# Block two's operand from rows short of the norms' rstd, the overflow loop moved ahead, and two sets of fillers

## The chip, the cores and the metric

One core of a Trainium2 chip runs the kernel. It has TensorE (PE: matmuls and transposes), VectorE (DVE), ScalarE (ACT), GpSimd (POOL) and SyncE (SP, which issues the DMAs here). The metric is the device time of one execution in microseconds (us), lower is better.

## The reference, cut to what matters

Two blocks on 512 tokens of width 1024, all float32. Block one is a token mixer (short convolution and forgetting attention with 16 heads, both gated) and a two-level mixture of 32 experts; its last step is an RMS norm. Block two is an mLSTM and pooling layer, which begins with an RMS norm of its own, and then a latent attention layer with 8 heads.

```python
x = x + token_mixer(rmsnorm(x, norm_mix_g), ...)
x = x + hier_moe(rmsnorm(x, norm_ffn_g), ...)
return rmsnorm(x, norm_final_g)                  # end of block one
...
u = rms_norm(x, a_norm_g) @ a_w_in               # start of block two
xm, om, gates, zm, xp, zp = jnp.split(u, ...)
...
p = softmax(where(mask, q @ k.T * scale, -inf))  # latent attention, per head
o = (p @ v) * silu(z)
```

Two RMS norms follow each other at the seam: block two's operand is x times a factor per row (both norms' rstd) times a gain per column (norm_final_g times a_norm_g).

## The kernel before, in words

Each float32 operand of a dense product is split into a high part rounded to float32r (on ACT) and a low part (the difference, on DVE or POOL); `hilo` and `wsplit` do this, and `pair3` makes three matmuls of it. `dense_T` makes one 128 x 512 output tile from 24 such matmuls (8 blocks of k, three each) into a PSUM bank of the group `mm`. Weights come by DMA into tiles `raw`, and their two parts into two buffers `w`.

The instructions of an engine run in a fixed order that a planner wrote down ahead, with the program order as its first rule of choice and its own costs and waits. `pin` and `in_order` keep matmuls in program order; `no_sync_barrier` keeps all that stands behind it behind all that stands ahead; `issue_after` holds work back until a given instruction. `banks` says which PSUM banks a group (mm, tr, s, o, c) rotates over.

Attention of block one (`attention`) runs 8 pairs of heads, with scores in bank group s, `softmax_T` and value products (L452). Behind it `gate_att` makes 8 gate tiles with `dense_T` and a tanh on ACT (L477) into one tile `sg` whose pool is opened after attention's pool is closed. PE uses these gate products to fill its waits as far as banks allow.

Experts are run in 16 pairs (`experts`). The last steps there: the down products of pair 15 in two halves (`down_half`, L848), `combine` (L923, added to the rows X by DVE, L924) in two halves, and between them `overflow`, a loop with a count read from memory, which runs no iteration with these inputs (L1027, L1028). All five engines meet at it. Then `final_half` takes the statistics per tile and half: X times norm_final_g on POOL into `hs` (L947), the squares on ACT (L948, L951) or DVE (L953). `final_rows` makes both norms' rstd from them (L958 on), scales the rows (L967, L969), `front` transposes the scaled rows (L252) and splits them into the operand `hT` of block two, and POOL makes the new X from hs (L1173).

Block two's first part is `gates_m` (24 matmuls with 36 columns), `pool_branch` (8 pairs of dense tiles xp and zp) and `mlstm` (4 heads, each with two dense blocks om, two tiles xm, two tiles zm). An output of xp or xm is copied by ACT (L1248, L1291), one of zp or zm goes to `silu2` (tanh on ACT, product on DVE, L1180 and L1181). From xm the convolution on DVE (L1297) leads to xc, the operand of the q and k products.

In the latent attention `scores` makes 32 units (head, tile): a maximum on DVE (L1628), its product with the query's scale on DVE (mx, L1629), the exponential on ACT (L1632), the reciprocal on DVE (L1634) and the scaling of the row on DVE for even and on POOL for odd tiles (L1635); `values` transposes the result (L1649) and multiplies it with V (L1656). The weights uq and uk of the next heads are split in one piece each (L234, L235).

Of the kernel before, what the change touches and what calls it, by code (L numbers as in the profile page):

```python
# [19 lines left out]
P = 128  # L20
# [16 lines left out]
GATES_FIRST = 4  # L37
ROUTER_AT = (1, 2, 3, 4, 5, 6)
GAIN_ON_ACT = (0, 1)
# [6 lines left out]
class Program:  # L46
# [427 lines left out]
    def gate_att(self):  # L474
        for f in range(KB):
            pg = self.dense_T(self.hT)
            self.nc.scalar.activation(self.sg[:, f, :], pg, AF.Tanh, scale=0.5)  # L477

    def mix_out(self, pool):
        nc = self.nc  # L480
        sg = self.sg
        for f in range(KB):
            py = self.dense_T(self.by_k(self.B))
            m = pool.tile([P, T], F32, name="m2", bufs=2)
            nc.vector.scalar_tensor_tensor(m, sg[:, f, :], 1.0, py, op0=OP.add, op1=OP.mult)
# [308 lines left out]
    def experts(self):  # L794
# [133 lines left out]
    def begin_final(self, n):  # L928

        nc = self.nc  # L930
        s = [self.moe_slots[(n + i) % MOE_SLOTS]() for i in range(7)]
        two = lambda u: [u[:, 0:D], u[:, D:2 * D]]
        self.hs = two(s[0]) + two(s[1])
        self.rows = two(s[2]) + two(s[5])
        self.gfin, self.gfin2 = two(s[3])
        self.sq = [s[4][:, i * 512:(i + 1) * 512] for i in range(NT)]
        self.y_over = [x.bitcast(F32R) for x in two(s[6])]
        nc.sync.dma_start(self.gfin, self.a["norm_final_g"].to_broadcast([P, D]))
        nc.gpsimd.tensor_tensor(self.gfin2, self.gfin, self.gfin, op=OP.mult)
        self.ss = self.small.tile([P, 2, NT, 2], F32, name="s12", bufs=1)  # L940

    def final_half(self, t, half):

        nc = self.nc
        c = slice(half * 512, half * 512 + 512)
        x, q = self.X[:, t, c], self.sq[t]
        nc.gpsimd.tensor_tensor(self.hs[t][:, c], x, self.gfin[:, c], op=OP.mult)  # L947
        self.squared = nc.scalar.activation(q, x, AF.Square, accum_out=self.ss[:, half, t, 0:1])  # L948
        gain = self.ss[:, half, t, 1:2]
        if half == 0 and t in GAIN_ON_ACT:  # L950
            nc.scalar.activation(q, self.hs[t][:, c], AF.Square, accum_out=gain)  # L951
        else:
            nc.vector.scalar_tensor_tensor(q, q, 1.0, self.gfin2[:, c], op0=OP.mult, op1=OP.mult, accum_out=gain)  # L953

    def final_rows(self):

        nc = self.nc
        nc.vector.tensor_tensor(self.ss[:, 0], self.ss[:, 0], self.ss[:, 1], op=OP.add)  # L958
        v, w = (self.small.tile([P, NT, 2], F32, name="v12", bufs=1), self.small.tile([P, NT], F32, name="v2", bufs=1))
        nc.vector.tensor_scalar(v[:, :, 0], self.ss[:, 0, :, 0], 1.0 / D, EPS, op0=OP.mult, op1=OP.add)  # L960
        nc.vector.tensor_scalar(w, v[:, :, 0], EPS, None, op0=OP.mult)
        nc.vector.scalar_tensor_tensor(v[:, :, 1], self.ss[:, 0, :, 1], 1.0 / D, w, op0=OP.mult, op1=OP.add)
        r = self.rsqrt(v.rearrange("p t n -> p (t n)"), 8)
        for t in range(NT):
            g = r[:, 2 * t + 1:2 * t + 2]
            if t == 3:
                nc.scalar.activation(self.rows[t], self.hs[t], AF.Copy, scale=g)  # L967
            else:
                nc.vector.tensor_scalar(self.rows[t], self.hs[t], g, None, op0=OP.mult)  # L969
        self.rfin = r  # L970
# [123 lines left out]
    def block_one(self):  # L1094
# [6 lines left out]
        with ExitStack() as s1:  # L1101
# [20 lines left out]
            self.sg = sgp.tile([P, KB, T], F32, name="sg")  # L1122
            self.gate_att()
# [41 lines left out]
            self.expert_banks()  # L1165
            for _ in steps:
                pass
            self.final_rows()
            self.usual_banks()
            self.hT = self.by_k(self.B)  # L1170
            self.front(self.rows, self.hT, "a_norm_g")
            for t in range(NT):
                nc.gpsimd.tensor_scalar(self.X[:, t, :], self.hs[t], self.rfin[:, 2 * t:2 * t + 1], None, op0=OP.mult)  # L1173
# [3 lines left out]
    def silu2(self, pool, src, out):  # L1177

        nc = self.nc
        nc.scalar.activation(out, src, AF.Tanh, scale=0.5)  # L1180
        nc.vector.scalar_tensor_tensor(out, out, 1.0, src, op0=OP.add, op1=OP.mult)  # L1181

    def gates_m(self, pool, keep):
# [7 lines left out]
        for k in range(KB):  # L1191
            self.pair3(b[:36, :], (wgh[:, k, :], wgl[:, k, :]), self.hT[k],
                       k == 0, k == KB - 1)
        it, ft, e, cf, ones = (pool.tile([4, T], F32, name="gm_" + n) for n in ("i", "f", "e", "cf", "one"))
# [31 lines left out]
    def pool_branch(self, pool, first):  # L1226
# [11 lines left out]
        for g in range(4):  # L1238
# [4 lines left out]
            for j in range(2):  # L1243
# [4 lines left out]
                nc.scalar.copy(x[:, 16:], px)  # L1248
# [11 lines left out]
                self.silu2(pool, pz, sz[:, j, :])  # L1260
# [11 lines left out]
    def mlstm(self, pool):  # L1272
# [7 lines left out]
        for h in range(4):  # L1280
            th = pool.tile([P, NT, 256], F32, name="th_om", bufs=1)
            for u, b in self.two_blocks():
                nc.scalar.activation(th[:, 2 * u:2 * u + 2, :], b, AF.Tanh, scale=0.5)
# [21 lines left out]
            for j in range(2):  # L1305
                self.silu2(pool, self.dense_T(self.hT), sz[:, j, :])
# [108 lines left out]
    def block_two_a(self):  # L1415
        nc, tc = self.nc, self.tc
        with ExitStack() as s1:
# [105 lines left out]
    def mla_heads(self, p, keep, x3):  # L1523
# [4 lines left out]
        def q_tile(hp, t):  # L1528
            d = pairs[hp]
            if t == 0:  # L1530
# [4 lines left out]
                self.hilo(*d["uq"], w[:, :1152], lo_engine=nc.gpsimd if hp else None)  # L1535
# [11 lines left out]
        def kv_tile(hp, t):  # L1547
            d = pairs[hp]
            if t == 0:
# [4 lines left out]
                self.hilo(*d["uk"], w[:, :1024], lo_engine=nc.gpsimd if hp else None)  # L1554
# [63 lines left out]
        def scores(h, t):  # L1618
# [10 lines left out]
            nc.vector.tensor_tensor(mx, mx, qs, op=OP.mult)  # L1629
# [5 lines left out]
            (nc.gpsimd if t % 2 else nc.vector).tensor_scalar(pr[:, :nk], pr[:, :nk], rp, None, op0=OP.mult)  # L1635
# [113 lines left out]
VEC_NAMES = [("norm_mix_g", 8), ("norm_ffn_g", 8), ("conv_w0", 8), ("conv_w1", 8), ("conv_w2", 8), ("conv_b", 8), ("b_forget", 1),  # L1749
# [32 lines left out]
def layout(i):  # L1782
# [35 lines left out]
    vecs[:16, VEC_AT["b_forget"]] = i["b_forget"]  # L1818
    o["norm_final_g"] = i["norm_final_g"].reshape(1, D)
# [51 lines left out]
```

## Time and profile before

| what | value |
|---|---|
| median of 3 runs | 1791.58 us (1791.04 to 1791.61) |
| the profiled execution's own time | 1791.53 us |
| its span, first to last instruction | 1789.8 us |
| mean granted TensorE clock | 0.988 |
| busy: PE, DVE, ACT, POOL | 1718.7, 908.2, 616.0, 314.2 us |
| DMA moved | 321.35 MB |

Times in the profile count from the first instruction of the span. An engine's busy time leaves out its waits; where an engine sat idle, a timeline row gives in brackets how long, and which engine's instruction ended it. The granted clock is a share of TensorE's full speed: 1.00 is 2.4 GHz, 0.50 is 1.2 GHz.

### The profile page before, as it was taken

The page shows a single profiled execution, that of the slowest core. Times are in us where ns is not written, and L with a number is a line of the kernel's source. Part 1 is how long each engine was busy: PE and PEld are TensorE (multiplying, and loading weights), DVE is VectorE, ACT ScalarE, POOL GpSimd, SP SyncE. Part 2 cuts the span into 40 slices and gives each one's busy share as a digit, 9 for nine tenths or more (in the row PEclk, how much of TensorE's full clock was granted, in tenths as well). Part 3 has the DMA queues.
Part 4 walks back from the last instruction along what each step waited for, and adds up shares of the span by engine and source line. Part 5 has one row for each costly group of instructions (what it writes and reads, how often), then busy time and mean ns, then how long its engine had stood idle before and what let it go on. Part 6 is the DMA issues. An engine that isn't in the chain of part 4 may idle for free. (4 is left out here: it accounts for less than half of the span.)

```text
span 1789.8 us, 22587 instructions
## 1 busy us (share of the span) xinstructions
PE 1718.7 (96%) x8762; PEld 1250.6 (70%) x8762; DVE 908.2 (51%) x1832; ACT 616.0 (34%) x1236; POOL 314.2 (18%) x285
## 2 busy tenths in 40 slices
PE   7999999999899999999999994999999999998988
PEld 5788888788688644445444532788888887987877
DVE  7833224545245343434343436665367677635672
ACT  3422225555333111011101112433244445554661
POOL 2310025344210000000000005110011110033542
PEclk9999999999899999999999997999999999999999
DMA  5122233433325789999999982122221222321202
GB/s 195 71 94 94 94 107 119 138 117 113 118 94 194 285 359 421 418 419 418 421 420 419 420 351 98 47 81 108 89 89 66 89 71 90 133 84 61 71 24 83
DMA packets 52844, 321.35 MB, mean 180 GB/s; under 512 B 7264, under 2 KB 7776, under 8 KB 17408
## 3 DMA queue, kind: packets, MB, share of 16 engines
q1 hardware_dynamic: 52736, 319.90, 46.3%
q8 instruction: 70, 1.15, 0.3%
q14 instruction: 38, 0.31, 0.1%
HBM read 310.37 MB, written 4.19 MB: 176 GB/s over the span
## 5 line engine op out<-in xcount | busy, mean ns | idle before, releaser
L146 DVE TENSOR_TENSOR w<-raw,w 128x1024 fp32r<-128x1024 f32 (+3 forms) x144 | 181.4, 1261 | 155.3 <-ACT w L143 154.4
L143 ACT CAST w<-raw 128x1024 fp32r<-128x1024 f32 (+3 forms) x160 | 161.8, 1012 | 189.7 <-PE b L162 179.1
L160 PE MATMUL b<-B,w 128*128 128x512 f32 x484 | 191.5, 398 | 0.4 <-ACT B L237 0.4
L162 PE MATMUL b<-B,w 128*128 128x512 f32 x484 | 190.9, 396 | 0.8 <-DVE w L146 0.8
L161 PE MATMUL b<-B,w 128*128 128x512 f32 x484 | 191.5, 396 | 0.0
L160 PE MATMUL b<-hT,w 128*128 128x512 f32 x376 | 148.3, 394 | 1.2 <-ACT sg L477 1.2
L162 PE MATMUL b<-hT,w 128*128 128x512 f32 x376 | 147.8, 394 | 0.1
L161 PE MATMUL b<-hT,w 128*128 128x512 f32 x376 | 147.1, 391 | 0.0
L811 PE MATMUL b<-raw,xe 128*64 128x512 f32 x592 | 130.9, 594 | 0.0
L160 PEld LDWEIGHTS b<-B,w 128*128 128x128 f32 x484 | 91.5, 189 | 22.1 <-issue 1.3
L162 PEld LDWEIGHTS b<-B,w 128*128 128x128 f32 x484 | 91.4, 189 | 22.2 <-DVE w L146 1.7
L161 PEld LDWEIGHTS b<-B,w 128*128 128x128 f32 x484 | 91.4, 189 | 20.7 <-issue 0.2
L811 PEld LDWEIGHTS b<-raw,xe 128*64 128x64 f32 x592 | 41.5, 137 | 80.8 <-issue 78.7
L401 POOL TENSOR_SCALAR p<-p,rs 128x128 f32<-128x128 f32 (+3 forms) x64 | 69.0, 1087 | 120.4 <-DVE rs L400 104.5
L819 POOL CAST sel<-eye 128x256 fp32r<-128x256 f32 x16 | 7.0, 435 | 464.4 <-PE b L824 406.3
L987 ACT ACTIVATE th_e<-b,hr 128x512 f32<-128x512 f32 x16 | 11.0, 687 | 214.4 <-PE b L811 202.7
L160 PEld LDWEIGHTS b<-hT,w 128*128 128x128 f32 x376 | 70.7, 188 | 17.8 <-issue 1.6
L162 PEld LDWEIGHTS b<-hT,w 128*128 128x128 f32 x376 | 70.6, 188 | 16.2 <-issue 0.8
L924 DVE TENSOR_TENSOR X<-X,b 128x512 f32<-128x512 f32 x128 | 78.6, 679 | 3.9 <-PE b L923 3.9
L161 PEld LDWEIGHTS b<-hT,w 128*128 128x128 f32 x376 | 70.7, 188 | 13.7
L923 PE MATMUL b<-y,gT 128*128 128x512 f32 x256 | 69.1, 411 | 7.1 <-DVE y L238 4.1
L238 DVE SCALAR_TENSOR_TENSOR y<-b,ws,y 128x512 fp32r<-128x512 f32 x32 | 24.0, 751 | 95.7 <-ACT y L237 92.4
(608 smaller groups left out, 3666.9 us busy)
## 6 DMA issues: line engine op xcount, KB each, us to landing
raw<-moe SPq DMA_DIRECT2D x110, 1024.0 KB, 12.9
raw<-wT SPq DMA_DIRECT2D x63, 1024.0 KB, 4.8
hT<-moe SPq DMA_DIRECT2D x52, 1024.0 KB, 12.9
w<-moe SPq DMA_DIRECT2D x28, 1024.0 KB, 13.3
raw<-wR SPq DMA_DIRECT2D x16, 1024.0 KB, 4.8
raw<-w_out_T SPq DMA_DIRECT2D x4, 1024.0 KB
raw<-w_qkv SPq DMA_DIRECT2D x4, 768.0 KB
raw<-w_uq SPq DMA_DIRECT2D x4, 576.0 KB, 5.1
```

Of the source, the lines that this page charges most:

```text
L143: self.nc.scalar.copy(h, raw)
L146: self.last_split = (lo_engine or eng).tensor_sub(l, raw, h.bitcast(F32))
L160: nc.tensor.matmul(out, lh, rh, start=start, stop=False)
L161: nc.tensor.matmul(out, lh, rl, start=False, stop=False)
L162: return nc.tensor.matmul(out, ll, rh, start=False, stop=stop)
L238: return nc.vector.scalar_tensor_tensor(lo, src, scale, hi.bitcast(F32), op0=OP.mult, op1=OP.subtract)
L401: nc.gpsimd.tensor_scalar(p[:, :nk], p[:, :nk], rs, None, op0=OP.mult)
L811: last = self.pin(nc.tensor.matmul(b[rows[e], :], d["xe"][:, k, s0 + 64 * e:s0 + 64 * e + 64], w, start=k == 0, stop=k == KB - 1))
L819: nc.gpsimd.tensor_copy(sel.rearrange("p a (e s) -> p a e s", e=2), self.eye[:, :, 2 * pair:2 * pair + 2][:, :, :, None].to_broadcast([P, ...
L923: self.pin(self.nc.tensor.matmul(b, gT[:, t * P:(t + 1) * P], y[i][:, c], start=i == 0, stop=i == 1))
L924: nc.vector.tensor_add(self.X[:, t, c], self.X[:, t, c], b)
L987: nc.scalar.activation(th, bg, AF.Tanh, scale=hr)
```

## The change

It has four parts. First, the seam. `overflow` moves ahead of the last pair's down products. Both down halves then follow each other, and after each half of `combine` the 4 transposes of each of four feature blocks read X itself (`front_half`); the split multiplies by the product of both gains (`gain`), so that `hT` lacks only the rows' rstd. Three banks hold the transposes. All squares go to ACT. `final_rows` no longer scales rows; it keeps the combined rstd (`r12`) and makes the new X on POOL. Second, `block_two_a` spreads r12 over a tile rB (a diagonal tile times ones on PE, copied by ACT), and each output of block two's input product is multiplied by it: xp, xm, zp, zm and the gates on DVE, om through the scale of its tanh. The load of the first weights no longer waits for the squares. Third, `sg` becomes one tile per gate; the first two lie in a pool that is open during attention, and their products stand right behind it in its scope. Fourth, in the latent attention mx is multiplied on ACT, odd tiles are scaled on ACT, and uq and uk are split in three and two pieces.

```diff
+GATES_EARLY = 2
-GAIN_ON_ACT = (0, 1)
...
-            self.nc.scalar.activation(self.sg[:, f, :], pg, AF.Tanh, scale=0.5)
+            self.nc.scalar.activation(self.sg[f], pg, AF.Tanh, scale=0.5)
+            yield
...
-        down_half(n_pairs - 1, 0)
-        self.combine(d["gT"], d["y"], 0)
-        down_half(n_pairs - 1, 1)
-        self.in_order = False
         self.overflow(pool)
         self.tc.no_sync_barrier()
-        for t in range(NT):
-            self.final_half(t, 0)
-        self.combine(d["gT"], d["y"], 1, self.final_half)
+        self.banks(mm=(0, 1, 2), s=(0, 1), c=(5, 6, 7), tr=(3, 4, 2))
+        for half in range(2):
+            down_half(n_pairs - 1, half)
+        for half in range(2):
+            self.combine(d["gT"], d["y"], half, self.final_half)
+            self.front_half(half)
+        self.in_order = False
...
-        nc.gpsimd.tensor_tensor(self.gfin2, self.gfin, self.gfin, op=OP.mult)
+        self.gain = self.small.tile([P, KB], F32, name="gain", bufs=1)
+        o, u = VEC_AT["norm_final_g"], VEC_AT["a_norm_g"]
+        nc.vector.tensor_tensor(self.gain, self.vecs[:, o:o + KB], self.vecs[:, u:u + KB], op=OP.mult)
...
+        nc.gpsimd.tensor_tensor(h, x, self.gfin[:, c], op=OP.mult)
+        for i, src in enumerate((x, h)):
+            nc.scalar.activation(self.junk[i], src, AF.Square, accum_out=self.ss[:, half, t, i:i + 1])
+
+    def front_half(self, half):
+
+        for k in range(4 * half, 4 * half + 4):
+            b = self.bank("tr")
+            for t in range(NT):
+                self.pin(self.nc.tensor.transpose(b[:, t * P:(t + 1) * P], self.X[:, t, k * P:(k + 1) * P], self.ident))
+            self.hilo(*self.hT[k], b, scale=self.gain[:, k:k + 1])
...
+        self.r12, self.r12h = (self.small.tile([P, NT], F32, name=n, bufs=1) for n in ("r12", "r12h"))
+        nc.vector.tensor_copy(self.r12, r[:, :, 1])
+        nc.vector.tensor_scalar(self.r12h, r[:, :, 1], 0.5, None, op0=OP.mult)
         for t in range(NT):
-            g = r[:, 2 * t + 1:2 * t + 2]
-            if t == 3:
-                nc.scalar.activation(self.rows[t], self.hs[t], AF.Copy, scale=g)
-            else:
-                nc.vector.tensor_scalar(self.rows[t], self.hs[t], g, None, op0=OP.mult)
-        self.rfin = r
+            nc.gpsimd.tensor_scalar(self.X[:, t, :], self.hs[t], r[:, t, 0:1], None, op0=OP.mult)
...
+                self.sg = [gp.tile([P, T], F32, name=f"sg{f}") for f in range(GATES_EARLY)]
+                gate = self.gate_att()
+                for _ in range(GATES_EARLY):
+                    next(gate)
...
+        if r is not None:
+            x = pool.tile([P, T], F32, name=scratch, bufs=1)
+            nc.vector.tensor_tensor(x, src, r, op=OP.mult)
+            src = x
         nc.scalar.activation(out, src, AF.Tanh, scale=0.5)
         nc.vector.scalar_tensor_tensor(out, out, 1.0, src, op0=OP.add, op1=OP.mult)
...
-                nc.scalar.copy(x[:, 16:], px)
+                nc.vector.tensor_tensor(x[:, 16:], px, self.rB, op=OP.mult)
...
-                self.silu2(pool, pz, sz[:, j, :])
+                self.silu2(pool, pz, sz[:, j, :], self.rB)
...
-                nc.scalar.copy(x[:, 3:], px)
-                self.hilo(xm[0][:, j, :], xm[1][:, j, :], px)
+                nc.vector.tensor_tensor(x[:, 3:], px, self.rB, op=OP.mult)
+                self.hilo(xm[0][:, j, :], xm[1][:, j, :], x[:, 3:])
...
-                self.silu2(pool, self.dense_T(self.hT), sz[:, j, :])
+                self.silu2(pool, self.dense_T(self.hT), sz[:, j, :], self.rB, "ya")
...
-                with tc.issue_after(self.squared.ins):
-                    first = [self.next_T(nc.gpsimd) for _ in range(2)]
-                    self.gates_m(p, big)
+                first = [self.next_T(nc.gpsimd) for _ in range(2)]
+                self.rB = big.tile([P, T], F32, name="rB")
+                diag, ones = p.tile([P, NT, P], F32, name="diag"), p.tile([P, P], F32, name="ones")
+                nc.gpsimd.memset(ones, 1.0)
+                nc.vector.tensor_tensor(diag, self.ident[:, None, :].to_broadcast([P, NT, P]),
+                                        self.r12[:, :, None].to_broadcast([P, NT, P]), op=OP.mult)
+                b = self.bank("s")
+                nc.tensor.matmul(b, ones, diag.rearrange("p t c -> p (t c)"), start=True, stop=True)
+                nc.scalar.copy(self.rB, b)
+                self.gates_m(p, big)
...
-                self.hilo(*d["uq"], w[:, :1152], lo_engine=nc.gpsimd if hp else None)
+                for c in (slice(0, 384), slice(384, 768), slice(768, 1152)):
+                    self.hilo(*(x[:, c] for x in d["uq"]), w[:, c], lo_engine=nc.gpsimd if hp else None)
...
-            nc.vector.tensor_tensor(mx, mx, qs, op=OP.mult)
+            nc.scalar.activation(mx, mx, AF.Copy, scale=qs)
...
-            (nc.gpsimd if t % 2 else nc.vector).tensor_scalar(pr[:, :nk], pr[:, :nk], rp, None, op0=OP.mult)
+            if t % 2:
+                nc.scalar.activation(pr[:, :nk], pr[:, :nk], AF.Copy, scale=rp)
+            else:
+                nc.vector.tensor_scalar(pr[:, :nk], pr[:, :nk], rp, None, op0=OP.mult)
```

## Rows read from the trace of the kernel before

**Rows 1.** The page: busy us of the engines, and PE's 40 slices.

```profile
PE 1718.7 (96%) x8762; PEld 1250.6 (70%) x8762; DVE 908.2 (51%) x1832; ACT 616.0 (34%) x1236; POOL 314.2 (18%) x285
...
PE   7999999999899999999999994999999999998988
```

**Rows 2.** Windows: length, busy PE, PEld, DVE, ACT, POOL (instructions), PE clock, DMA share, GB/s.

```profile
460.00:480.00 20.00, 14.54 (x68) 9.73 (x67) 5.72 (x16) 8.38 (x19) 6.70 (x10) 0.74 0.21 75
...
1080.00:1100.00 20.00, 9.64 (x40) 4.19 (x36) 12.10 (x19) 9.72 (x24) 9.31 (x7) 0.90 0.40 158
1100.00:1120.00 20.00, 7.62 (x25) 5.42 (x25) 14.97 (x28) 3.10 (x4) 17.43 (x8) 0.50 0.17 61
...
1400.00:1420.00 20.00, 19.90 (x99) 16.23 (x98) 14.14 (x20) 8.95 (x15) 2.70 (x2) 1.00 0.30 106
...
1640.00:1660.00 20.00, 15.12 (x85) 12.94 (x83) 14.62 (x43) 11.76 (x34) 10.14 (x7) 0.91 0.22 69
...
1720.00:1740.00 20.00, 15.69 (x97) 13.30 (x97) 12.49 (x33) 10.96 (x23) 11.30 (x8) 1.00 0.04 14
```

**Rows 3.** Timeline of PE at the seam: start, us, what, idle before and its releaser.

```profile
1077.85 3.65 PE L848 MATMUL b<-w,aT 128*64 128x512 f32 x16 [1.61 <-DVE X L924]
...
1090.83 2.11 PE L923 MATMUL b<-y,gT 128*128 128x512 f32 x8 [2.22 <-DVEq L1028]
...
1111.20 0.69 PE L252 MATMUL b<-ident,raw 128*128 128x128 f32 x2 [18.25 <-DVE raw L969]
...
1123.27 0.60 PE L252 MATMUL b<-ident,raw 128*128 128x128 f32 x4
...
1131.04 0.39 PE L160 MATMUL b<-B,wgh 128*36 128x512 f32 x1
```

**Rows 4.** Timeline of the same stretch, the other engines.

```profile
1073.53 4.27 DVE L924 TENSOR_TENSOR X<-X,b 128x512 f32<-128x512 f32 x7 [0.23 <-PE b L923]
...
1103.43 2.18 DVE L958 TENSOR_TENSOR s<-s 128x8 f32<-128x8 f32 x1
...
1124.62 0.75 DVE L238 SCALAR_TENSOR_TENSOR B<-b,vecs,B 128x512 fp32r<-128x512 f32 x1 [1.08 <-ACT B L237]
...
1123.90 0.69 ACT L237 ACTIVATE B<-b,vecs 128x512 fp32r<-128x512 f32 x1 [1.14 <-PE b L252]
...
1090.69 12.15 POOL L947 TENSOR_TENSOR hT<-X,raw 128x512 f32<-128x512 f32 x8 [19.63 <-DVEq L1028]
...
1110.45 12.24 POOL L1173 TENSOR_SCALAR X<-hT,rq_z 128x1024 f32<-128x1024 f32 x4 [2.57 <-DVE rq_z L186]
...
1090.54 0.33 SPq L137 DMA_DIRECT2D raw<-wT  x1
```

**Rows 5.** Timeline at the end of attention, PE and ACT.

```profile
470.15 4.54 PE L452 MATMUL b<-pT,v 128*64 128x256 f32 x24 [0.68 <-ACT pT L405]
...
475.22 1.58 ACT L477 ACTIVATE sg<-b 128x512 f32<-128x512 f32 x3
```

**Rows 6.** Timeline: a product like rB's in block one, and a head of mLSTM.

```profile
43.86 1.28 DVE L318 TENSOR_TENSOR cu<-b,rstd 128x512 f32<-128x512 f32 x2
...
1407.87 0.62 ACT L234 CAST xc<-sx 128x512 fp32r<-128x512 f32 x1 [1.70 <-DVE sx L1301]
...
1408.73 0.40 PE L160 MATMUL b<-xc,w 128*128 128x512 f32 x1
```

**Rows 7.** Groups of instructions by line and shape: count, busy us, mean ns, idle before.

```profile
L1629 DVE TENSOR_TENSOR mx<-mx,ss 128x1 f32<-128x1 f32 x32 | 9.6, 303 | 0.1
...
L1635 POOL TENSOR_SCALAR p<-p,rs 128x512 f32<-128x512 f32 x8 | 12.5, 1567 | 15.3 <-DVE rs L1634 15.3
...
L267 ACT ACTIVATE mx<-ident 128x1 f32<-128x1 f32 x1 | 0.2, 203 | 0.0
```

**Rows 8.** Timeline in the latent attention, DVE and POOL.

```profile
1639.60 2.31 DVE L1629 TENSOR_TENSOR mx<-mx,ss 128x1 f32<-128x1 f32 x1
...
1639.49 2.40 POOL L235 TENSOR_TENSOR uk<-raw,uk 128x1024 fp32r<-128x1024 f32 x1 [2.54 <-ACT uk L234]
```

More of the change, by code (lines that the diff above doesn't have):

```diff
@@ L930, in begin_final @@
         nc = self.nc
-        s = [self.moe_slots[(n + i) % MOE_SLOTS]() for i in range(7)]
+        s = [self.moe_slots[(n + i) % MOE_SLOTS]() for i in range(5)]
         two = lambda u: [u[:, 0:D], u[:, D:2 * D]]
         self.hs = two(s[0]) + two(s[1])
[L934 to L937, printed above, removed]
+        self.gfin = s[3][:, :D]
+        self.junk = [s[2][:, i * 512:(i + 1) * 512].bitcast(BF)[:, :512] for i in range(2)]
+        self.y_over = [x.bitcast(F32R) for x in two(s[4])]
         nc.sync.dma_start(self.gfin, self.a["norm_final_g"].to_broadcast([P, D]))
-        nc.gpsimd.tensor_tensor(self.gfin2, self.gfin, self.gfin, op=OP.mult)
+        self.gain = self.small.tile([P, KB], F32, name="gain", bufs=1)
+        o, u = VEC_AT["norm_final_g"], VEC_AT["a_norm_g"]
+        nc.vector.tensor_tensor(self.gain, self.vecs[:, o:o + KB], self.vecs[:, u:u + KB], op=OP.mult)
         self.ss = self.small.tile([P, 2, NT, 2], F32, name="s12", bufs=1)
@@ L945, in final_half @@
         c = slice(half * 512, half * 512 + 512)
[L946 to L951, printed above, removed]
-        else:
-            nc.vector.scalar_tensor_tensor(q, q, 1.0, self.gfin2[:, c], op0=OP.mult, op1=OP.mult, accum_out=gain)
+        x, h = self.X[:, t, c], self.hs[t][:, c]
+        nc.gpsimd.tensor_tensor(h, x, self.gfin[:, c], op=OP.mult)
[7 more added lines that the diff above has]
+            self.hilo(*self.hT[k], b, scale=self.gain[:, k:k + 1])
     def final_rows(self):
@@ L1120, in block_one @@
                 self.pool_lo = 0
+                self.sg = [gp.tile([P, T], F32, name=f"sg{f}") for f in range(GATES_EARLY)]
+                gate = self.gate_att()
+                for _ in range(GATES_EARLY):
+                    next(gate)
             sgp = gates.enter_context(tc.tile_pool(name="gates", bufs=1, reuse_waits="tile"))
-            self.sg = sgp.tile([P, KB, T], F32, name="sg")
-            self.gate_att()
+            self.sg += [sgp.tile([P, T], F32, name=f"sg{f}") for f in range(GATES_EARLY, KB)]
+            for _ in gate:
+                pass
             with tc.tile_pool(name="mix", bufs=1, reuse_waits="tile") as p:
@@ L1165, in block_one @@
             self.expert_banks()
+            self.hT = self.by_k(self.B)
             for _ in steps:
@@ L1169, in block_one, with silu2 @@
             self.usual_banks()
[L1170 to L1173, printed above, removed]
         rp.close()
-    def silu2(self, pool, src, out):
+    def silu2(self, pool, src, out, r=None, scratch="silu_x"):
         nc = self.nc
+        if r is not None:
+            x = pool.tile([P, T], F32, name=scratch, bufs=1)
+            nc.vector.tensor_tensor(x, src, r, op=OP.mult)
+            src = x
         nc.scalar.activation(out, src, AF.Tanh, scale=0.5)
@@ L1193, in gates_m @@
                        k == 0, k == KB - 1)
+        g = pool.tile([36, T], F32, name="gm_g")
+        nc.vector.tensor_tensor(g, b[:36, :], self.rB[:36, :], op=OP.mult)
+        b = g
         it, ft, e, cf, ones = (pool.tile([4, T], F32, name="gm_" + n) for n in ("i", "f", "e", "cf", "one"))
@@ L1282, in mlstm @@
             for u, b in self.two_blocks():
-                nc.scalar.activation(th[:, 2 * u:2 * u + 2, :], b, AF.Tanh, scale=0.5)
+                for i in range(2):
+                    nc.scalar.activation(th[:, 2 * u + i, :], b[:, i], AF.Tanh, scale=self.r12h[:, 2 * u + i:2 * u + i + 1])
             xm = [pool.tile([P, 1280], F32R, name=f"xmw{i}", bufs=1)[:, :1024].rearrange("p (j t) -> p j t", j=2)
@@ L1553, in kv_tile @@
                 d["uk"] = [keep.tile([P, 1024], F32R, name=f"uk{i}", bufs=1) for i in range(2)]
-                self.hilo(*d["uk"], w[:, :1024], lo_engine=nc.gpsimd if hp else None)
+                for c in (slice(0, 512), slice(512, 1024)):
+                    self.hilo(*(x[:, c] for x in d["uk"]), w[:, c], lo_engine=nc.gpsimd if hp else None)
             q = slice(t * P, (t + 1) * P)
```

8 lines of the change are left out of this document (4 added, 4 removed).

## The prediction

> **What bounds the kernel now.** I read three views in this order. First the page's busy shares and its 40 slices [rows 1]: TensorE (PE) is busy 96% of 1789.8 us, and one slice, the 25th (1074 to 1119 us), shows a 4 among nines. So time is to be won only where PE stands still, runs at its low clock, or has less to do. Second, the busy time in windows of 20 us [rows 2]: three places have holes. At the end of block one's attention (460 to 480) PE works 14.54 of 20 and its clock is 0.74 in the mean. At the handover from the experts to block two (1080 to 1120) it works 9.64 and 7.62 of 40, and in the second half the clock is 0.50, the lower of its two levels (1.2 instead of 2.4 GHz). In the latent attention (1640 to 1660, 1720 to 1740) it works 15.12 and 15.69. In the mLSTM (1400 to 1420) there is no hole: PE 19.90, with VectorE (DVE) at 14.14 the next fullest engine. Third, the timeline of the handover [rows 3, 4]: after the last combine products at 1090.83 (2.11 long) PE has nothing until 1111.20, 18.25 us, because the transposes read rows that wait for the norms' rstd: eight gain products on POOL, the squares, the sum at 1103.43 and what follows it on DVE. The transposes and the first dense matmuls then start at half clock.
>
> **Part 1, the handover.** I compare the moment from which block two's dense matmuls run as if without a gap. Before: the 24 gate matmuls begin at 1131.04 behind two dense products of 24 matmuls. One matmul takes 0.228 (3.65 for 16 [rows 3]), 48 take 10.9, so the dense work started as if at 1120.1.
> After, step by step. DVE's adds of pair 14 end at 73.53 + 4.27 = 1077.80 as before [rows 4]. The overflow loop now stands here. Its exit cost PE an idle of 2.22 at 1090.83, the wait for DVE's last instruction included; here DVE is already the last, and 1.61 us were idle anyway in front of 1077.85, so I let PE start at 1078.5 (bounds 1078.0 and 1080.1). Two down halves: 2 x 3.65, to 1085.8. First combine, 2.11, to 1087.9. The four DVE adds at 4.27/7 = 0.61 with one low half (0.75) between them end near 1089.7, so PE waits 1.8. Eight groups of four transposes at 0.60: 4.8. One wait for a transpose bank (three banks, evacuated by 0.69 on ACT and 0.75 on DVE) 0.6. Second combine 2.11; the wait for its adds is filled by dense matmuls over the first half of the features, whose operands are ready by then. Sum: 1078.5 + 7.3 + 2.11 + 1.8 + 4.8 + 0.6 + 2.11 = 1097.2. The gain is at most 1120.1 - 1097.2 = 22.9. I take 20, since the waits between 1088 and 1097 can bring the low clock on once (about 3 us of work doubled); lower bound 10, below as rival A.
> What moves with it: the first weight load, issued at 1090.54 right behind the loop, goes out some 12 us earlier and is hidden. The eight POOL products (12.15, or 1.52 each) leave PE's path, but the statistics still need them, and the rstd is needed by everything that takes an output of block two. Its row rB: POOL from 1086.5 at 1.52 each ends near 1098.7; from the sum at 1103.43 to the first transposes at 1111.20 the old chain took 7.8; the broadcast matmul and a copy take about 2; so near 1109. PE needs it when all three banks of dense outputs are full: three dense products and the gates, 96 x 0.228 = 21.9 after 1097.2, at 1119. The cover is 10 us; with it gone, the loss is what exceeds it. Dropped row scalings, gfin2 and the four POOL products of 12.24 lie beside PE either way.
>
> **Part 2, two gates early.** Between 460 and 480 PE idles 5.46, and 0.26 x 2 x 20 = 10.4 us pass at half clock [rows 2]. In these lie the 24 value products (4.54, at full clock 2.27) and some ten of the last transposes (0.60 for four at full clock [rows 3], so 1.5 lost). Together 5.46 + 2.27 + 1.5 = 9.2. The hole is there because ScalarE (ACT) can't empty the three gate outputs until attention's buffers are free: three tanh in a row at 475.22 [rows 5]. With two tiles outside that pool, two more products of 24 can run: 2 x 24 x 0.228 = 10.9, more than the hole. The later gates' work shrinks by as much. I take 8, bounds 4 and 9.2. An earlier end here also moves the expert loads, whose slots PE itself frees, so it's not lost there.
>
> **Part 3, rstd on the outputs of block two.** 16 multiplications replace ACT copies and 16 are new, 32 on DVE; the same operation (dense output times a row) took 1.28/2 = 0.64 [rows 6]: 20.5 us. Without cover that is the loss; the cover is DVE's idle time, 5.9 of 20 [rows 2]. The exposed place is the start of each of four mLSTM heads: ACT's cast of xc waited for DVE (1.70, at 1407.87) and PE's first product with it stands at 1408.73 [rows 6]. One or two multiplications, 0.64 to 1.3 us, slip in ahead of it. I take 0.75 x 4 = 3 us lost, bounds 0 and 20.5, nearer the low end since PE lost 0.1 of 20 there.
>
> **Part 4, the latent softmax.** The [128x1] multiplication mx takes 9.6 us on DVE, 0.303 each, against about 0.15 when undisturbed [rows 7, 8]; one took 2.31 while POOL worked on uk from 1639.49 for 2.40. On ACT the nearest row, also [128x1], took 0.203: 32 make 6.5. Half of the row scalings go from POOL (1.567 for 128x512) to ACT, where a 128x512 pass took 0.69 [rows 4]: shorter waits for the transposes, some 10 us more on ACT. uq and uk in pieces shorten the blocks that others queue behind. The two windows shown idle 4.88 + 4.31 = 9.2. I take 4 won, bounds -4 (ACT, at 11.76 of 20, becomes the later one) and +9.2.
> On mx the Trainium skill, SBUF — State Buffer, section "Who interferes with whom", says that a DVE instruction with two SBUF inputs blocks while a GpSimd instruction that reads SBUF has the shared port. The trace agrees [rows 8]: mx ended 0.02 us after POOL's uk. By that rule the change also makes a new victim: the diagonal tile for rB has two SBUF inputs and meets POOL's row products (12.24 for four). It would wait up to 3.06 us, which rival A holds.
>
> **Sum.** 20 + 8 - 3 + 4 = 29. The profiled execution took 1791.53 (span 1789.8, 1.7 around it), 0.05 below the median of 1791.58: 1791.5 - 29 = 1762.5.
>
> **Rivals.** A: the handover's gain is half given back. rB is late: two weight halves on POOL go ahead of the gain products, the two small DVE operations behind them wait as the sum at 1103.43 did (2.18), and the diagonal waits for a POOL product of 3.06 as mx waited for POOL [rows 8]; PE stands in its fixed order at the broadcast matmul, and its clock falls once more. About 7 late plus 3 at low clock: 10 lost, 1772.5. For it speaks that the order is fixed ahead, against it the cover of 10.
> B, slower: DVE becomes the bound in block two. If each of the 32 outputs holds its bank so long that PE waits t, the loss is 32 t; the other parts win 32, so it decides from t = 1.0 us. With one blocked DVE operation of 2.31 ahead of each: 74 lost, 1791.5 - 32 + 74 = 1833. Against it: a bank may be emptied up to 24 x 0.228 = 5.5 us late, and DVE idles 30%.
> C: the change doesn't do what it says: the transposes stay behind the norms and the two gates aren't used as fillers. Then only parts 3 and 4 are left, -3 + 4: 1790.5, within what can be told. Against it: no operand of the transposes is a norm's output any more.
> D: everything takes its good bound: 22.9 + 9.2 - 0 + 9.2 = 41, 1750.5.
>
> **How the numbers follow.** Chances: the forecast (its own range 1756 to 1769) 0.63; A (1769 to 1778) 0.18; D (1750 to 1756) 0.13; C 0.03; B 0.03. The prediction is 1762.5. The range 1753 to 1774 takes the forecast, about 0.6 of A and half of D: 0.8. A difference under 0.2% (3.6 us) can't be told from none. Faster: 0.63 + 0.18 + 0.13 = 0.94; same 0.03 (C); slower 0.03 (B).
>
> **What would show it.** Part 1: the idle of 18.25 is gone, the first dense matmul of block two stands near 1095 less what part 2 won, and the low clock of 1100 to 1120 with it; a PE wait for the broadcast matmul would show A. Part 2: dense gate matmuls between the last value products, window 460 to 480 near 20 at clock 1.00. Part 3: PE idle at the xc products of each head of 0.7 us; several us would be B's way. Part 4: no mx above 0.3 us and less idle from 1640 to 1740. The prediction is wrong if rB or ACT's queue takes PE's place as the last to be ready.

## The result, and the profile after

The changed kernel takes 1770.01 us (median of 4 runs, 1768.14 to 1772.66) against 1791.31 (1790.86 to 1791.61): a ratio of 0.9882, 95% interval 0.9865 to 0.9900, so 21.1 us faster (17.9 to 24.2). The forecast was 29 won, 1762.5, range 1753 to 1774. The profiled execution took 1768.14, its span 1766.3.

The page of after: busy time, and PE in 40 slices. The 4 of [rows 1] is gone.

```profile
PE 1715.1 (97%) x8764; PEld 1246.9 (71%) x8764; DVE 905.1 (51%) x1825; ACT 629.5 (36%) x1300; POOL 292.2 (17%) x278
PE   7999999999999999999999999999999999999999
```

Busy time in windows of 20 us of after (columns: PE, PEld, DVE, ACT, POOL with their instructions, granted clock, DMA share, GB/s).

```profile
460.00:480.00 20.00, 17.54 (x100) 13.89 (x99) 7.97 (x17) 9.53 (x20) 6.80 (x10) 1.00 0.16 57
1100.00:1120.00 20.00, 17.40 (x74) 11.75 (x72) 9.73 (x18) 8.82 (x12) 15.74 (x6) 1.00 0.15 52
1120.00:1140.00 20.00, 18.37 (x74) 13.47 (x73) 17.04 (x29) 9.10 (x12) 0.00 (x0) 0.91 0.16 54
1320.00:1340.00 20.00, 18.56 (x78) 14.06 (x77) 18.90 (x26) 8.88 (x14) 2.82 (x2) 1.00 0.26 92
1620.00:1640.00 20.00, 17.18 (x99) 15.13 (x98) 14.30 (x47) 17.13 (x52) 6.74 (x5) 0.91 0.20 66
1640.00:1660.00 20.00, 19.73 (x117) 17.69 (x116) 14.38 (x52) 16.32 (x56) 11.16 (x12) 1.00 0.29 91
```

The attention's end runs at full clock, and the handover no longer leaves a slice empty [rows 2]. New holes stand at 1100 to 1140, behind the handover, and in the mLSTM heads, where DVE is now full: 18.90 of 20, and PE lost 1.44. In the latent attention ACT is now the fullest engine beside PE.

Five moments that both timelines show say where the time was won and given back:

| moment | before | after | earlier by |
|---|---|---|---|
| DVE's adds of pair 14 end | 1077.80 | 1070.44 | 7.4 |
| first output gate of mLSTM on ACT | 1279.14 | 1255.31 | 23.8 |
| first scores of the latent attention | 1633.01 | 1615.73 | 17.3 |
| last head's output y on DVE | 1758.61 | 1733.63 | 25.0 |
| end of the span | 1789.75 | 1766.27 | 23.5 |

Part 2 won 7.4, part 1 some 16.4, the mLSTM lost 6.5, the latent attention won 7.7 and the last projection gave 1.5 of it back: behind the last y, PE still has 127 matmuls to do in after, 116 in before.

The handover on PE, timeline of after (start, duration, in brackets the idle time before and its releaser); it answers to [rows 3].

```profile
1071.01 3.65 PE L849 MATMUL b<-w,aT 128*64 128x512 f32 x16 [2.13 <-DVEq L1032]
1078.03 2.24 PE L924 MATMUL b<-y,gT 128*128 128x512 f32 x8
1083.70 0.74 PE L160 MATMUL b<-B,w 128*128 128x512 f32 x2 [0.50 <-ACT B L237]
...
1098.59 0.40 PE L160 MATMUL b<-B,wgh 128*36 128x512 f32 x1
...
1105.76 1.02 PE L1447 MATMUL b<-diag,ones 128*128 128x512 f32 x2
...
1114.52 0.47 PE L160 MATMUL b<-B,w 128*128 128x512 f32 x1 [2.60 <-DVE xp L1261]
1121.29 0.73 PE L160 MATMUL b<-mh,w 128*128 128x512 f32 x2 [0.94 <-ACT mh L234]
1122.58 0.38 PE L1224 MATMUL b<-ident,gm_i 4*128 4x4 f32 x4 [0.56 <-DVE gm_i L1215]
```

The same stretch on the other engines [rows 4].

```profile
1066.17 4.27 DVE L925 TENSOR_TENSOR X<-X,b 128x512 f32<-128x512 f32 x7 [0.23 <-PE b L924]
1100.10 0.69 DVE L1444 TENSOR_TENSOR diag<-ident,r 128x512 f32<-128x512 f32 x1
1113.09 0.68 DVE L1205 TENSOR_TENSOR gm_g<-b,rB 36x512 f32<-36x512 f32 x1 [9.14 <-ACT rB L1448]
1111.95 0.62 ACT L143 CAST w<-raw 128x512 fp32r<-128x512 f32 x1 [10.01 <-PE b L162]
1112.48 0.58 ACT L1448 COPY rB<-b 128x512 f32<-128x512 f32 x1
1100.06 12.17 POOL L974 TENSOR_SCALAR X<-hT,rq_z 128x1024 f32<-128x1024 f32 x4 [6.45 <-DVE r L971]
1112.20 3.60 POOL L146 TENSOR_TENSOR w<-raw,w 128x1024 fp32r<-128x1024 f32 x2
```

Up to 1111.75 the handover is as good as the best bound of the forecast. By then 96 dense matmuls are in the trace, the 24 of the gates among them; 96 x 0.2333 = 22.4, so they ran as if started at 1089.3, 18.9 behind the adds' end, where before it was 1120.1 - 1077.8 = 42.3. That is 23.4 won. But rB comes late in two steps. The diagonal is there at 1100.79, yet its broadcast stands behind the gates' products in PE's order and starts at 1105.76. PE has made it by 1106.8, and it is copied only at 1112.48: in ACT's fixed order the cast of pool_w's first part stands ahead of the copy, and it waits 10.01 us for PE to free a weight buffer. DVE waits 9.14 for rB, PE's banks fill, PE stops 2.60, 0.94 and 0.56, and the clock falls to 0.91 in the next window.

A head of the mLSTM, timeline of after: the second block's conv, xc, and qT [rows 6].

```profile
1383.72 0.68 DVE L1188 TENSOR_TENSOR ya<-b,rB 128x512 f32<-128x512 f32 x1
1386.52 0.74 DVE L1311 SCALAR_TENSOR_TENSOR cacc<-xpad,half,cacc 128x512 f32<-128x512 f32 x1
1388.61 0.62 ACT L143 CAST w<-raw 128x512 fp32r<-128x512 f32 x1 [0.69 <-PE b L162]
1389.13 0.62 ACT L234 CAST xc<-sx 128x512 fp32r<-128x512 f32 x1
1391.16 0.50 PE L161 MATMUL b<-xc,w 128*128 128x512 f32 x1 [0.43 <-POOL xc L235]
1393.30 0.50 PE L160 MATMUL b<-xc,w 128*128 128x512 f32 x1 [0.93 <-DVE qT L235]
```

Before, ACT's second cast of xc stood 0.86 ahead of PE's first product with xc [rows 6]; here it stands 0.78 behind it (that product began at 1388.35 with the first half). The first three heads, each from its first output gate to the next head's, are 51.81, 53.44 and 53.44 long, before 50.67, 51.47 and 51.39.

### The profile page after: what moved, and what is told of

Its sections match the earlier page's. It is cut to its first block, busy times and chain, and to the rows that moved or that the text cites. A ratio compares the mean times of both kernels' runs of the same rounds, so it can differ in the third digit from the quotient of the medians.

```text
span 1766.3 us, 22624 instructions
## 1 busy us (share of the span) xinstructions
PE 1715.1 (97%) x8764; PEld 1246.9 (71%) x8764; DVE 905.1 (51%) x1825; ACT 629.5 (36%) x1300; POOL 292.2 (17%) x278
## 5 line engine op out<-in xcount | busy, mean ns | idle before, releaser
L160 PEld LDWEIGHTS b<-hT,w 128*128 128x128 f32 x376 | 70.7, 188 | 17.3 <-issue 1.6
L162 PEld LDWEIGHTS b<-hT,w 128*128 128x128 f32 x376 | 70.6, 188 | 16.4 <-issue 0.8
L146 POOL TENSOR_TENSOR w<-raw,w 128x1024 fp32r<-128x1024 f32 (+1 forms) x16 | 36.4, 2280 | 228.3 <-ACT w L143 194.6
```

Of the source, the lines that this page charges most:

```text
L146: self.last_split = (lo_engine or eng).tensor_sub(l, raw, h.bitcast(F32))
L160: nc.tensor.matmul(out, lh, rh, start=start, stop=False)
L162: return nc.tensor.matmul(out, ll, rh, start=False, stop=stop)
```

## Experiments

Every run was timed in five rounds against the kernel before, on the same chip as it; the runs stand on four chips, on which the kernel before took 1790.7 to 1791.7. Gains are worked out as (1 - ratio) x 1791. A variant of after is told from after only where its runs lie outside 1768.1 to 1772.7.

**e1, part 2 alone.** The diff's lines for `GATES_EARLY`, `gate_att`, `sg` and `mix_out`, put into the kernel before.

> The kernel before with part 2 alone (the two early gates). Theory, from the trace of after, where the DVE adds of the last pair end 7.36 us earlier than before: 7.4 us faster, near 1784, with the window 460 to 480 at the full clock and near 17.5 busy. Rival: the expert stage is paced by its loads and takes the gain back by its end, 1790 to 1791.5, with the last adds ending near 1077.8 as before.

1784.36; ratio 0.9964 [0.9950, 0.9977], 6.5 won (4.1 to 9.0), the medians 7.3 apart. The window of e1, and the last pair's adds in its timeline:

```profile
460.00:480.00 20.00, 17.54 (x100) 13.93 (x99) 7.90 (x17) 10.06 (x21) 6.79 (x10) 1.00 0.20 64
```

```profile
1065.86 4.27 DVE L926 TENSOR_TENSOR X<-X,b 128x512 f32<-128x512 f32 x7 [0.23 <-PE b L925]
```

The hole is filled at full clock, and the adds of the last pair end 7.67 earlier than before, 600 us later: nothing of it was lost in the experts.

**e2, part 4 alone.** The diff's lines in `q_tile`, `kv_tile` and `scores`, put into the kernel before.

> The kernel before with part 4 alone (mx and the odd row scalings on ACT, uq and uk in pieces). Theory, from the distance between the first scores and the last output in the two traces, which is 6 us shorter after: 5 to 6 us faster, near 1786. Rival: the 6 us came from the different phase in which the stage was entered (loads and POOL work stand elsewhere against the scores), and part 4 alone is within 2 us of before.

1787.90; ratio 0.9975 [0.9964, 0.9987], 4.5 won (2.3 to 6.5). That lies between the theory (5 to 6) and the rival (within 2); the interval leaves out the rival and not the theory. In the profile the last y is 5.65 earlier than before with the scores begun within 0.1, but the end of the span only 3.5: the last projection gives 2.2 back, as in after, with the same 127 matmuls left behind the last y.

**e3, parts 1 and 3.** After without parts 2 and 4.

> The kernel before with parts 1 and 3 (operand from rows short of rstd, overflow loop ahead, rstd on the outputs) and neither the gates nor the latent softmax. Theory, from the traces: the handover gives 16.4 and the mLSTM takes 7.2, so 9 us faster, near 1782. Rival: the parts are not additive, because the expert loads that part 2 sends earlier are what lets the handover run without a wait; then this kernel is within 4 us of before, and after's 21 us need both.

1781.85; ratio 0.9948 [0.9935, 0.9962], 9.3 won (6.8 to 11.6). With e1 and e2: 6.5 + 4.5 + 9.3 = 20.3, after 21.1. The parts add up within their intervals; the rival falls.

**e4, rB copied by DVE.**

```diff
-                nc.scalar.copy(self.rB, b)
+                nc.vector.tensor_copy(self.rB, b)
```

> After, with the one copy of rB from its bank moved from ACT to DVE. Theory: rB was ready 5.7 us late only because ACT stood in its fixed order at a weight cast that waited for PE to free a buffer; without it the three PE waits of 2.60, 0.94 and 0.56 and the half clock after them go, 4 to 6 us faster than after, near 1765. Rival: the cast was not what counted, since the gates and the first product are bound by DVE's own queue once rB is there; then within 1.5 us of after, near 1770, with PE waits of the same sum in 1110 to 1127.

1770.11; ratio 0.9884 [0.9869, 0.9899]: no gain. Timeline of e4, three engines:

```profile
1108.21 0.69 DVE L1448 COPY rB<-b 128x512 f32<-128x512 f32 x1 [4.05 <-PE b L1447]
1113.26 4.04 POOL L146 TENSOR_TENSOR w<-raw,w 128x1024 fp32r<-128x1024 f32 x2
1115.66 0.50 PE L162 MATMUL b<-B,w 128*128 128x512 f32 x1 [1.89 <-POOL w L146]
```

rB's copy starts 4.3 us earlier and the waits for xp and mh are gone, but PE now stops for the low half of a weight that stands on POOL behind the four products that scale X. In after it stood there too (1112.20), hidden by the wait for xp. My theory of one late thing fell, the rival named the wrong engine: two things were late together.

**e7, rB on DVE and that low half on DVE.**

```diff
                 self.pool_lo = POOL_LO_BRANCH
+                self.lo_turn = 5
...
-                nc.scalar.copy(self.rB, b)
+                nc.vector.tensor_copy(self.rB, b)
```

> After, with rB copied by DVE (as in the run that moved only this copy and won nothing) and the turn of the low halves shifted, so that the second dense weight of the pool branch is halved by DVE and not by POOL behind the four products of 12.2 us. Theory: two things were ready at the same time near 1114, rB and this low half, and either alone gains nothing; with both gone PE's waits from 1110 to 1128 (4.1 us in after, 2.7 with rB alone) fall under 1, the half clock there goes, and it is 3 to 6 us faster than after, 1764 to 1767. Rival: the next thing in line (ACT's cast of pool_w, which waits for PE, with the gates' logarithms behind it) takes their place, within 1.5 us of after.

1769.86; ratio 0.9878 [0.9862, 0.9894]: within 1.5 us of after, the rival. The shifted turn moves later low halves too: POOL has one of 2.49 us between 1120 and 1140, where in after it has none. Timeline of e7:

```profile
1113.15 0.62 ACT L143 CAST w<-raw 128x512 fp32r<-128x512 f32 x1 [10.00 <-PE b L162]
1119.60 0.68 DVE L198 SCALAR_TENSOR_TENSOR gm_f<-gm_f,gm_e 4x512 f32<-4x512 f32 x1 [1.56 <-ACT gm_e L197]
1121.15 0.74 PE L160 MATMUL b<-mh,w 128*128 128x512 f32 x2 [2.44 <-ACT mh L234]
```

The cast of pool_w, the same that stood ahead of rB's copy in after, is third in the row: the gates' ACT work stands behind it, DVE waits for its logarithm ahead of the mix, and PE for mh.

**e9, and the cast behind the logarithm.** e7 with:

```diff
-        nc.scalar.activation(e, e, AF.Ln, bias=1.0)
+        self.gates_log = nc.scalar.activation(e, e, AF.Ln, bias=1.0)
...
-            ph, pl = self.wsplit(pw[:, g * 512:(g + 1) * 512], 512)
+            with ExitStack() as order:
+                if g == 0:
+                    order.enter_context(self.tc.issue_after(self.gates_log.ins))
+                ph, pl = self.wsplit(pw[:, g * 512:(g + 1) * 512], 512)
```

> The kernel with rB copied by DVE and the early low halves on DVE, and now with ACT's cast of pool_w's first part issued behind the gates' logarithm. In the run without that edit ACT waited at this cast from 1103.15 to 1113.15 for PE, the gates' ACT work began at 1113.68 although its input was there at 1110.0, DVE waited 1.56 for the logarithm ahead of the mix of the pool branch, and PE waited 2.44 for mh. Theory: this was the last of the row of things that were late together; PE's waits from 1110 to 1128 (3.0 there) fall under 1.2 and it is 2 to 4 us faster than after, 1766 to 1768. Rival: DVE's own work between rB and mh (the prefix sums of 128x512, the gates' scan) is as long as what PE has left, so the wait at mh stays above 1.5 and it is within 1.5 us of after.

1765.56, all runs from 1764.9 to 1765.7; ratio 0.9858 [0.9842, 0.9875], 25.4 won, 4.3 more than after. All of PE's waits from 1095 to 1140 in e9 (us in total, times, longest), and in its timeline ACT's start of the gates:

```profile
PE b L160 <- ACT mh L234: 0.8, 1, 0.8
PE b L1224 <- DVE gm_i L1215: 0.6, 1, 0.6
```

```profile
1109.48 0.72 ACT L1209 ACTIVATE gm_i<-gm_g,vecs 4x512 f32<-4x512 f32 x1 [6.90 <-DVE gm_g L1205]
```

The waits fell from 4.1 in after to 1.4 (the theory wanted less than 1.2 from 1110 on), the gates' work starts 4.2 earlier than in e7, and the time is a little below the theory's 1766 to 1768: the theory in the main. It beats both kernels. Moving this cast alone, which would also have freed rB's copy on ACT, was not run: whether all three edits are needed is open.

**e10, the overflow loop between down products and combine.** In after, `self.overflow(pool)` with its barrier and `self.banks(...)` moved behind the loop over `down_half`.

> After, with the overflow loop between the last pair's down products and its combine in place of ahead of the down products. Theory: in after the loop's exit lies under DVE's adds of the pair before (PE waited 2.13 there, 0.57 of it after their end), here PE has nothing beside it: 2 to 4 us slower than after, 1772 to 1774, with a PE wait of some 2 us for the loop's branch behind the down products. Rival: PE waits for DVE's adds in either order, since the loop only takes the place of the wait; within 1 us of after.

1770.11; ratio 0.9885 [0.9869, 0.9902]: not to be told from after, the rival's time. Timeline of e10:

```profile
1070.35 3.65 PE L849 MATMUL b<-w,aT 128*64 128x512 f32 x16 [1.61 <-DVE X L925]
1079.66 3.68 PE L924 MATMUL b<-y,gT 128*128 128x512 f32 x8 [2.23 <-DVEq L1032]
```

But the loop doesn't only take the place of the wait: PE's waits for adds and exit are 3.84 here and 2.13 in after, and the combine behind them takes 3.68 in place of 2.24, at a granted clock of 0.84 from 1080 to 1090 (after 1.00). Of these some 3 us, 0.9 are left at the first output gate of the mLSTM (185.8 behind the adds' end, in after 184.9), too little to show in the times. Between these two places of the loop no difference can be told; the place that it had before, ahead of the second half of combine, was not tried with the new operand.

**e5, mLSTM without rB.** The heads' part of part 3 undone, so that xm and zm lack the rows' rstd: it prices these multiplications and is no kernel to use.

```diff
-                nc.vector.tensor_tensor(x[:, 3:], px, self.rB, op=OP.mult)
-                self.hilo(xm[0][:, j, :], xm[1][:, j, :], x[:, 3:])
+                nc.scalar.copy(x[:, 3:], px)
+                self.hilo(xm[0][:, j, :], xm[1][:, j, :], px)
...
-                self.silu2(pool, self.dense_T(self.hT), sz[:, j, :], self.rB, "ya")
+                self.silu2(pool, self.dense_T(self.hT), sz[:, j, :])
```

> After, with the 16 multiplications by rB in the four mLSTM heads left out: the x products go to their buffer by an ACT copy and their halves are taken from the bank, as before, and SiLU reads the bank (what follows is computed from operands without rstd). Theory: of the 7.2 us that the four heads are longer in after, 4.6 are PE's waits at the first products with xc and with qT, because DVE's conv of the second feature block comes 1 to 2 us later; they go with the multiplications. The other 2.5 us are a slower spacing of the dense matmuls (0.2333 against 0.2289 us each), which stays or goes by itself. So 4 to 7 us faster than after, 1763 to 1766, heads 50.7 to 51.5 long. Rival: the heads are longer because ACT's fixed order puts a weight cast ahead of the xc cast, whatever DVE does; then under 2 us, 1768 to 1771.

1764.28, all runs below 1765.5; ratio 0.9850 [0.9833, 0.9866]: 5.7 faster than after. The window of e5 that answers to the one of after:

```profile
1320.00:1340.00 20.00, 20.00 (x85) 15.50 (x84) 16.08 (x23) 10.39 (x17) 2.70 (x2) 1.00 0.19 69
```

PE has no hole, DVE is down from 18.90 to 16.08, the heads are 51.02, 51.73 and 51.73 long. Part 3 in the heads costs it: the multiplications, and with them the copy of x, which they take over from ACT, and xm's halves, which wait for their output in place of the bank.

**e6, xm's low half on POOL.**

```diff
-                self.hilo(xm[0][:, j, :], xm[1][:, j, :], x[:, 3:])
+                self.hilo(xm[0][:, j, :], xm[1][:, j, :], x[:, 3:], lo_engine=nc.gpsimd)
```

> After, with the low half of xm (8 subtractions of 0.68 us, now between two SBUF tiles) on POOL in place of DVE. Theory of DVE's load: DVE's chain to the second conv is shorter by 0.7 to 1.4 us in each head and POOL is idle there, 2 to 4 us faster than after, 1766 to 1768. Rival, the shared port: each POOL subtraction of some 1.4 us stops a conv tap of DVE that reads two SBUF tiles, as POOL's xc at 1389.83 stopped DVE's szm at 1390.32 (1.34 in place of 0.68), and the tap ends later than if DVE had done the subtraction itself; then 1 to 4 us slower than after, 1771 to 1774, with taps of 1.3 us and more.

1772.23 (1769.3 to 1773.3); ratio 0.9894 [0.9878, 0.9911]: not faster; 2 slower by the medians, with overlapping runs. Timeline of e6:

```profile
1375.12 1.32 DVE L1308 TENSOR_SCALAR cacc<-xpad,half 128x512 f32<-128x512 f32 x1
1381.15 1.58 DVE L1315 SCALAR_TENSOR_TENSOR sx<-sx,cacc 128x512 f32<-128x512 f32 x1
1375.06 1.09 POOL L235 TENSOR_TENSOR xmw<-xpad,xmw 128x512 fp32r<-128x512 f32 x1 [18.81 <-ACT xmw L234]
1380.84 1.35 POOL L235 TENSOR_TENSOR xmw<-xpad,xmw 128x512 fp32r<-128x512 f32 x1 [4.69 <-ACT xmw L234]
```

Each DVE instruction that starts behind such a subtraction (0.54 and 0.69 alone) ends 0.3 to 0.5 behind POOL's end: DVE gave 0.68 away and lost 0.8 to 0.9. Over the four heads it gave away 5.5 us and lost 6.3 in the conv and its SiLU.

**e8 and e11, the two halves of part 4's moves undone.** In after, the odd row scalings back on POOL (e8), or mx back on DVE (e11).

> After, with the odd row scalings of the latent softmax back on POOL (mx stays on ACT, uq and uk in pieces). Theory: part 4 pays by mx and the pieces, and ACT, at 16 to 17 of 20 us busy there, is not relieved by the scalings; 0 to 3 us faster than after, 1767 to 1770. Rival: the scalings (1.57 us on POOL, 0.69 on ACT) are what part 4 pays by; then 2 to 4 us slower, 1772 to 1774.

> After, with mx multiplied on DVE again (the odd row scalings stay on ACT, uq and uk in pieces). Part 4 alone gave 3.8 us, and putting the scalings back on POOL lost 2.1. Theory: the rest, 1.5 to 2 us, is mx, which waited on DVE behind POOL's port (2.31 us once, 0.303 in the mean against 0.15): 1.5 to 2.5 us slower than after, 1771.5 to 1772.5. Rival: with the scalings off POOL and uk in pieces nothing blocks mx for long, so it is within 1 us of after, or faster, since ACT is the fuller engine there.

e8: 1772.29 (1771.0 to 1775.4), ratio 0.9894 [0.9878, 0.9911], 2 slower by the medians, as the rival said, but with overlapping runs. e11: 1774.03 (1771.4 to 1774.8), ratio 0.9904 [0.9887, 0.9920], 3.9 slower, one run of four inside after's: more than the theory's 1.5 to 2.5. Together they are 6.0 against part 4's 4.5 (2.3 to 6.5), so mx seems to count for the larger part; at this noise neither share is settled. Timeline of e11:

```profile
1667.49 1.43 DVE L1652 TENSOR_TENSOR mx<-mx,ss 128x1 f32<-128x1 f32 x1
1667.01 1.90 POOL L1606 TENSOR_TENSOR krow<-krow,ss 128x1024 f32<-128x1024 f32 x1 [5.90 <-DVE ss L1604]
```

Against the rival, something still blocks mx: three of the 32 take 1.1 to 1.4, this one ending 0.01 behind POOL's instruction. From 1590 to 1770 ACT waits 18.6 us for mx in e11 and 25.1 in before; in after, where mx is its own work, it waits 9.3 for the maximum.

**e12, e9 with the conv first.** In each head SiLU's multiplications behind the last tap, the cast of the v weights behind xc.

```diff
+                pz = self.dense_T(self.hT)
+                with self.tc.issue_after(tap.ins):
+                    self.silu2(pool, pz, sz[:, j, :], self.rB, "ya")
...
+            with self.tc.issue_after(low.ins):
+                ops.append(self.wsplit(qkv[:, 1024:1536], 512))
```

> The kernel with rB on DVE, the early low halves on DVE and the pool_w cast behind the logarithm (1765.6), and in each mLSTM head SiLU's multiplications by rB issued behind the last conv tap and the cast of the v weights behind xc. Theory: in after the second xc is late by the SiLU multiplication of 0.68 that stands ahead of DVE's last tap and by the weight cast of 0.62 that stands ahead of ACT's xc cast; 1.2 us earlier in each head, PE's waits for xc and qT (6.5 us in sum from 1240 to 1470) fall to 1 to 3, and it is 2 to 4 us faster than that kernel, 1761.5 to 1763.5. Rival: the waits at qT come from the chain bank, ACT cast, DVE subtraction of qT itself, which is as long whenever xc comes; then within 1 us, 1764.5 to 1766.5, with PE's waits at qT still 0.9 in each head.

1765.13 (1764.7 to 1770.0); ratio 0.9863 [0.9847, 0.9879]: not to be told from e9. PE's longest wait in the mLSTM of e12 (us in total, times, longest):

```profile
PE b L160 <- DVE qT L235: 2.8, 3, 0.9
```

In its profile the three heads are 51.02, 52.85 and 52.82 long, 2.0 less in sum than e9's, and the waits for xc's low half are gone; the 0.9 at qT stays in three of four heads, as the rival said. But not for the rival's reason: in the first head, with the same chain, there is no wait. ACT's casts of qT in e12, first and second head:

```profile
1284.59 0.59 ACT L234 CAST qT<-b 128x512 fp32r<-128x512 f32 x1 [0.81 <-PE b L162]
1336.18 1.07 ACT L234 CAST qT<-b 128x512 fp32r<-128x512 f32 x2 [1.09 <-PE b L162]
```

In the first head the casts of qT's two halves start 1.40 apart (the other at 1283.19); in the others they stand back to back, because PE ends the two banks within some 0.5, and has no product of the second left to do while the chain empties the first. So it is in every head: in before and e5 the casts are 1.4 to 1.7 apart, with no wait, and in after and e9 they are back to back, with a wait of 0.9. No run moved this order alone.

## Why the prediction was right, and where it was off

The direction and the range held; the gain was 8 smaller than the 29. That the range held is in part luck: 1770.0 lies outside the forecast's own 1756 to 1769 and just inside rival A's 1769 to 1778, of which the range had taken a part. And the last sign that the prediction named for being wrong came: rB, held up in ACT's queue, took PE's place as the last to be ready. Parts 2 and 4 went as told, part 1 up to 1111.75; the cover of rB and the price of part 3 did not.

**Part 2, +8:** 6.5 (4.1 to 9.0) in e1, and 7.4 to 7.7 by the timelines. Right, and not lost in the loads.

**Part 1, +20:** e3's 9.3 and e5's 5.7 make 15. Two steps were off, in opposite directions. The dense work began better than forecast: 23.4 against my sum's 22.9, since it starts between the transposes at full clock, with waits of 0.27 to 0.50 in place of the 1.8 and 0.6. But the step "so near 1109", rB with a cover of 10 us, failed. PE needed rB when I said: 1119 less the 7.4 of part 2 is 1111.6, and PE stopped at 1111.75. rB came at 1113.06, not at 1101.6 (1109 less 7.4). I had followed POOL and DVE, but not what stands ahead of the broadcast on PE (5.0 from the diagonal's end to its start, which alone would have left rB in time) nor ahead of the copy on ACT (5.7). Rival A had the consequence (PE stands, the clock falls once more) with the wrong mechanism: the sum took 0.16 in place of 2.18, and the diagonal took 0.69 at 1100.10 though POOL's products began beside it at 1100.06, so the wait of up to 3.06 that the prediction gave it did not come (which of the two was first, rows 0.04 apart don't settle). Its loss of 10 was about 7 (23.4 less the 16.4 by which mLSTM was nearer): 4.1 of waits, some 1.8 for the half clock (0.09 of 20 us), the rest, by my reading, the slower matmuls told below. e4, e7 and e9 show that three orders stood behind one another, on ACT, POOL and ACT again: undoing the first alone or the first two gains nothing, all three 4.3.

**Part 3, -3:** mis-sized, 5.7. The place was right, the start of each head. I took 0.75 a head; it is 0.8 in the first and 1.7 in the others (53.44 against e5's 51.73), because the xc chain has a SiLU multiplication ahead of its last tap, and DVE, at 18.90 of 20, has no gap in which to make up for it. That order is worth 0.8, 0.6 and 0.6 by e12; what is left in the later heads, 1.1, is mostly the 0.9 at qT. Rival B, DVE as the bound everywhere, did not come: the waits sit only at xc and qT.

**Part 4, +4:** 4.5 (2.3 to 6.5). Right in sum. The 0.15 of an undisturbed mx stands in neither group of rows named for it, but it is right: 23 of the 32 took 0.14 to 0.16. One price was wrong: mx on ACT takes 0.301 in the mean, 9.2 for 32, not 0.203, so the sign of no mx above 0.3 did not come. Groups of after, to be read against [rows 7]:

```profile
L1652 ACT ACTIVATE mx<-mx,ss 128x1 f32<-128x1 f32 x32 | 9.2, 301 | 9.5 <-DVE mx L1651 9.3
```

The Trainium skill, ScalarE: Activation LUTs, section "What ACT_TABLE_LOAD costs", says that each [128,1] operand read through a pointer lengthens an activation by about 93 ns; the trace agrees, 0.301 against the 0.203 of [rows 7], 0.098 more. So the busy time did not get less by the move (9.6 on DVE, 9.2 on ACT); what pays, by e11, is that mx no longer stands in DVE's order, where POOL held some of it up; how much of the 3.9 that is, no run tells.

**Sum by runs:** 6.5 + 4.5 + 9.3 = 20.3, against 29 = 8 + 4 + 17. What was off lies almost whole in parts 1 and 3.

## What to carry to other kernels

When a value is moved off the path and becomes needed later, follow its last hop on the engine that copies it: what stands ahead of that copy in the fixed order, and whether that waits for the very engine the value is to feed. A wait that goes away may show another of the same length behind it; undo them together before saying that one doesn't matter. And room in the mean is no cover at one place: DVE, 70% busy here, took four more passes of 0.68 us in a head only at a loss of up to 1.7, since the chain to the next product ran through it without a gap.

## What the runs showed of the hardware

**Dense matmuls have two spacings.** Timeline rows of before (54 matmuls apart) and, below, of after (63 apart), the same operation at granted clock 1.00:

```profile
1154.00 0.40 PE L160 MATMUL b<-B,w 128*128 128x512 f32 x1
1166.37 0.39 PE L160 MATMUL b<-B,w 128*128 128x512 f32 x1
```

```profile
1134.86 0.40 PE L160 MATMUL b<-B,w 128*128 128x512 f32 x1
1149.56 0.40 PE L160 MATMUL b<-B,w 128*128 128x512 f32 x1
```

That is 0.2291 and 0.2333 us a matmul. Either spacing holds over tens of microseconds; in after the slower one lies over most of the handover and the mLSTM, and e5's heads, without a wait at xc or qT, are still 0.3 longer than before's. It doesn't go with the change: in the last projection DVE's adds, 24 matmuls apart, stand 5.60 apart at the end of before and 5.49 in after. What sets it is open; no run here was made for it.

**POOL stops a DVE instruction with one large input too.** In e6 the TENSOR_SCALAR at 1375.12 reads one 128x512 tile and took 1.32 in place of 0.54. The Trainium skill, SBUF — State Buffer, section "Who interferes with whom", counts such an instruction among those that can take both port pairs in its fast mode; the trace agrees. Over the eight blocks of the four heads this operation took 0.932 in the mean in e6 and 0.544 in after. Whether it is the same lock as at mx [rows 8], no run here tells.
